# Opening by feature blocks, output projection by token halves, one PSUM pool and a paced residual reload in a two-block transformer kernel

## Chip, cores and metric

One core of a Trainium2 chip runs the whole program. The metric is device time in microseconds (us) of that core for one execution.

## What is computed

Two transformer blocks on one sequence of 512 tokens, 1024 features wide, with a context of 256 tokens. Cut to what bears on the change:

```
# first block (norms are RMS norms, shift and scale come from silu(c) @ ada_w)
h  = norm(x) * (1 + scale1) + shift1          # hc the same from the context
q, k, v, gu, gv, ga, gb = split(h @ w_in)
k_c, v_c = hc @ w_in's columns of k and v
y_a = neighborhood_attention(q, k, v, k_c, v_c)  # 8 heads of 64
y_b = gelu(gu) * (ws @ layernorm(gelu(gv)) + bs) # spatial gating
m  = sigmoid(ga) * (y_a @ w_pa) + sigmoid(gb) * (y_b @ w_pb)
x  = x + g1 * (m @ w_out)
h2 = norm(x) * (1 + scale2) + shift2
# PEER: product keys pick 16 of 16384 experts per head and token
x  = norm(x + g2 * sum_e g_e * gelu(u_e . h2) * v_e)
# second block
x  = x + g * merge(sliding_window_attention(h), retention(h))
x  = x + swiglu(norm(x));  out = norm(x)
```

## The kernel before

Activations lie feature-major: a feature block is 128 features on the partitions by 512 tokens, and there are eight of them. Every float32 product is made of three products of reduced-width parts: `mm3` (L859) multiplies the high part by the high part, the high by the low and the low by the high. `weight` (L850) loads one 512 KB weight from a queue that SyncE (SP) issues in order (L852), splits off its high part on ScalarE (L854) and its low part on VectorE (L856) or, where `pool` is set, on GpSimd. Four raw buffers and three of each part let a weight be issued about six ahead of its use. `split` (L917) does the same for activations. `proj` makes one 512-wide output block from one weight: 8 feature blocks by 3 products, 24 matmuls. A scheduler of the language orders each engine's instructions by priority and readiness; each engine and each DMA queue then runs its list in that order.

**Opening** (`body`, L968 to L1055). The transposed input xT is loaded, `stats` squares it and `rfactor` (L883) makes the norm's factor R1 (Ln, Exp, Square on ScalarE, two VectorE operations nt and nR). The modulation weights adaA come in eight loads of 1 MB, one for each block of *input* features (L969 on), each split in two pieces (ah on ScalarE, al on VectorE). So the sums of all shifts and scales end together, with the last load:

```python
for k in range(KB):
    nc.sync.dma_start(ar, I["adaA"][k])
    ...
        nc.tensor.matmul(a_[:4, :], scp[:, k, :], ah[:, d], start=k == 0, stop=False)
        nc.tensor.matmul(a_[:2, :], scp[:, k, 0:2], al[:, d], start=False, stop=k == KB - 1)
```

Four copies to asb, sixteen transposes, m1 (L989, L990) and s1 (L998) follow, then `modulated` (L940): per feature block md on VectorE (L943), hh on ScalarE (L944), hl on VectorE (L945). The same is done for the context (cT, hc). Only then come the four projections of gv (a gelu on each, L1047, gv transposed at L1057 for the layernorm), then the four of gu.

**Attention** (L1188 to L1227). Four head pairs b, four query blocks each: scores S (L1194, L1195) into two banks, bias and maximum on VectorE, pr = exp on ScalarE (L1200), transposes T (L1203), output O (L1211). A list `beside[b]` names projections that fill TensorE's gaps between these: for b < 3 the next pair's queries, keys and values, and for every b two of the eight `gate` projections (L1071).

**Output projection** (L1246 to L1257). For each of eight output blocks: 24 matmuls, the residual block xr loaded through the ScalarE queue, x1 = acc * g1 + xr (L1255), `squares` (L902), whose sum over features is made by two matmuls with ones (L915). Then `rfactor`, and in `peer` md, hh, hl of h2 (L249 to L251) and the first three query projections together (`proj_many`, L254). x1 is kept in device memory as xs (L256).

**PEER** (`peer`, L137). After the retrieval, for each of 128 groups of experts, 24 hidden-layer matmuls; for the early groups the result `act` is written to device memory (`spilled`, L382) and read back by SP (`fetch`, L448) when its turn to be multiplied by the expert outputs comes (`output`, L427, which splits it as wh and wl and runs 18 matmuls into six banks o_ps). The gate tables (ring), expert weights (raw from in_uT, in_uv) and gathered rows (GpSimd queue) stream beside. `paced` (L159) makes an instruction wait for the output multiplication that was written last. At the end xr, all of xs, is reloaded for the residual (L475), ysb takes the six banks (L480, L482), and `block` (L485) transposes and adds, from about 1771 us on.

**PSUM.** Five pools one after another, each with its own tags and numbers of banks; a pool's banks become free for the next pool when the pool closes.

## Time and profile before

| | |
|---|---|
| median of 3 runs | 2605.16 us (2601.26 to 2610.33) |
| profiled execution's own time | 2605.44 us |
| its span in the trace | 2603.7 us |
| mean granted clock of TensorE | 0.982 |
| TensorE (PE) busy | 2494.0 us, 96% |
| VectorE (DVE) busy | 1793.4 us, 69% |
| ScalarE (ACT) busy | 1057.7 us, 41% |
| GpSimd (POOL) busy | 310.7 us, 12% |

The time of an execution holds 1.7 us around the span. PEld is TensorE's weight loading, which runs beside its matmuls. A row of the time order gives start, duration, engine, line, output and inputs, and in brackets how long the engine had been idle and the instruction that ended it. A window row gives busy times and, behind them, the granted clock of TensorE as a share of 2.4 GHz. All stretches are in us from the start of the span.

### The profile page before, as it was taken

What the parts mean: (1) busy time and instruction counts of PE and PEld (TensorE: products, weight loads), DVE (VectorE), ACT (ScalarE), POOL (GpSimd) and SP (SyncE); (2) the same over time, 40 slices, a digit from 0 to 9 for tenths busy, and PEclk for the clock granted to TensorE, in tenths of its full rate; (3) what the DMA queues carried; (4) which work ended last, traced back from release to release, by engine and by line L of the source; (5) the groups of instructions that cost most, each with busy time, mean ns of one, the idle gap of its engine ahead of it and who ended that gap; (6) DMA issues with size and microseconds to landing.
All of it is one profiled execution on the core that took longest, in us unless ns stands there. A gap on an engine that the chain in (4) does not pass through costs nothing.

```text
span 2603.7 us, 34186 instructions
## 1 busy us (share of the span) xinstructions
PE 2494.0 (96%) x12941; PEld 2128.5 (82%) x12941; DVE 1793.4 (69%) x2999; ACT 1057.7 (41%) x1820; POOL 310.7 (12%) x199
## 2 busy tenths in 40 slices
PE   5899999899899999999989999998999999999998
PEld 2688888689889999999968888886788888888887
DVE  6555655799998888868868888876765334533345
ACT  6424553333335444444433334434533323422343
POOL 1000110002531111122212222210000000000000
PEclk9899999999999999999989999999999999999999
DMA  6353433224677888899998899973112232222254
GB/s 251 109 170 121 146 105 119 85 90 145 214 247 280 300 294 292 293 334 345 332 323 309 312 359 351 362 267 105 57 42 76 94 97 98 96 96 96 95 181 164
DMA packets 145764, 511.24 MB, mean 196 GB/s; under 512 B 13632, under 2 KB 39360, under 8 KB 125888
## 3 DMA queue, kind: packets, MB, share of 16 engines
q1 hardware_dynamic: 114352, 330.14, 37.3%
q0 software_dynamic: 18432, 134.23, 14.2%
q10 hardware_dynamic: 12816, 44.70, 4.6%
q8 instruction: 101, 1.65, 0.3%
q14 instruction: 63, 0.52, 0.1%
HBM read 465.50 MB, written 43.52 MB: 195 GB/s over the span
## 4 chain that ended last, share of the span: by engine, by line
PE 84%; DVE 9%; ACT 2%; issue 1%; DMA 1%; POOL 0%; DVEq 0%; SPq 0%; ACTq 0%; POOLq 0%
PE ps_mm L860 13%; PE ps_mm L861 13%; PE ps_mm L862 13%; PE o_ps L862 6%; PE o_ps L861 6%; PE o_ps L860 6%; PE ps_S L861 3%; PE ps_S L860 3%; PE ps_S L862 3%; PE g_ps L196 3%; DVE lo L856 2%; PE acc L861 2%; PE acc L862 2%; PE acc L860 2%; PE ps_O L1211 1%
## 5 line engine op out<-in xcount | busy, mean ns | idle before, releaser
L856 DVE TENSOR_TENSOR lo<-raw,hi 128x1024 fp32r<-128x1024 f32 x474 | 592.3, 1250 | 388.7 <-ACT hi L854 375.7
L854 ACT ACTIVATE hi<-raw 128x1024 fp32r<-128x1024 f32 x478 | 504.1, 1056 | 775.7 <-PE ps_mm L861 455.9
L860 PE MATMUL ps_mm<-hh,hi 128*128 128x512 f32 (+1 forms) x1776 | 663.4, 375 | 26.7 <-ACT gv L1047 11.9
L862 PE MATMUL ps_mm<-hh,lo 128*128 128x512 f32 (+1 forms) x1776 | 658.7, 371 | 24.2 <-DVE lo L856 24.2
L861 PE MATMUL ps_mm<-hl,hi 128*128 128x512 f32 (+1 forms) x1776 | 660.2, 372 | 2.3 <-DVE hl L919 2.2
L860 PEld LDWEIGHTS ps_mm<-hh,hi 128*128 128x128 f32 x1776 | 337.8, 190 | 66.1 <-ACT gv L1047 12.3
L862 PEld LDWEIGHTS ps_mm<-hh,lo 128*128 128x128 f32 x1776 | 338.5, 191 | 63.9 <-DVE lo L856 27.8
L861 PEld LDWEIGHTS ps_mm<-hl,hi 128*128 128x128 f32 x1776 | 338.2, 190 | 41.3 <-DVE hl L919 3.3
L860 PE MATMUL o_ps<-hi,wh 128*128 128x512 f32 x768 | 300.1, 391 | 12.1 <-ACT wh L918 12.1
L177 POOL DMA_INDIRECT rows<-in_uv,dix x128 | 214.3, 1674 | 763.2 <-DVE act L434 190.0
L862 PE MATMUL o_ps<-hi,wl 128*128 128x512 f32 x768 | 300.4, 391 | 0.4 <-DVE wl L919 0.4
L861 PE MATMUL o_ps<-lo,wh 128*128 128x512 f32 x768 | 300.1, 391 | 0.0
L860 PEld LDWEIGHTS o_ps<-hi,wh 128*128 128x128 f32 x768 | 144.8, 189 | 42.1 <-ACT wh L918 12.5
L862 PEld LDWEIGHTS o_ps<-hi,wl 128*128 128x128 f32 x768 | 144.7, 188 | 32.1 <-DVE wl L919 2.0
L168 DVE SCALAR_TENSOR_TENSOR accn<-rows,wgt,accn 128x1024 f32<-128x1024 f32 x128 | 167.2, 1306 | 5.0 <-ACT wgt L174 3.5
L861 PEld LDWEIGHTS o_ps<-lo,wh 128*128 128x128 f32 x768 | 144.8, 189 | 29.6
L171 DVE SCALAR_TENSOR_TENSOR rows<-rows,hn 128x1024 f32<-128x1024 f32 x128 | 156.5, 1223 | 17.2 <-ACT act L380 8.3
L918 ACT ACTIVATE wh<-act 128x384 fp32r<-128x384 f32 x104 | 54.6, 526 | 256.4 <-PE o_ps L861 239.3
L192 DVE TENSOR_TENSOR gi<-oh,gt 128x1536 bf16<-128x1536 bf16 x96 | 91.3, 954 | 0.9
L190 DVE TENSOR_TENSOR oh<-iob,ji 128x1024 bf16<-128x1024 bf16 x96 | 65.8, 688 | 26.9 <-PE g_ps L196 26.2
L196 PE MATMUL g_ps<-gi,oh 128*128 128x128 bf16 x1152 | 77.5, 219 | 0.0
L196 PEld LDWEIGHTS <-oh 128*128 128x128 bf16 x1152 | 66.1, 97 | 10.4 <-issue 7.7
(400 smaller groups left out, 3530.7 us busy)
## 6 DMA issues: line engine op xcount, KB each, us to landing
raw<-in_uT SPq DMA_DIRECT2D x128, 512.0 KB, 5.0
raw<-in_uv SPq DMA_DIRECT2D x128, 512.0 KB, 6.5
raw<-in_win SPq DMA_DIRECT2D x82, 512.0 KB, 3.4
raw<-in_wd SPq DMA_DIRECT2D x44, 512.0 KB, 3.3
act<-act ACTq DMA_DIRECT2D x52, 384.0 KB, 3.4
act<-act SPq DMA_DIRECT2D x52, 384.0 KB, 7.7
gs<-stage ACTq DMA_DIRECT2D x16, 1152.0 KB, 6.8
ring<-gs SPq DMA_DIRECT2D x12, 1536.0 KB, 13.4
```

What stands on the lines that cost most here:

```text
L168: nc.vector.scalar_tensor_tensor(accn, rows.pop(k - 3)[:, D:], wgt[:, c], accn, op0=ALU.mult, op1=ALU.add)
L171: paced(nc.vector.scalar_tensor_tensor(r[:, :D], r[:, :D], 1.0, hn, op0=ALU.mult, op1=ALU.mult, accum_out=dot[:, c]))
L177: paced(nc.gpsimd.indirect_dma_start(out=r, out_offset=None, in_=I["uv"], in_offset=bass.IndirectOffsetOnAxis(ap=dix[:, k:k + 1], axis=0)))
L190: nc.vector.tensor_tensor(oh, io, each(ji[:, t0 // 4], 2), ALU.is_equal)
L192: nc.vector.tensor_tensor(gi, oh[:, 1].unsqueeze(1).broadcast_to([P, 3, 2, P, 2]), each(gt[:, t0 // 4], 3), ALU.mult)
L196: nc.tensor.matmul(g_ps[:, t, :], oh[:, 0, t // 2, :, t % 2], gi[:, j, t // 2, :, t % 2], start=j == 0, stop=j == 2)
L854: nc.scalar.activation(hi, raw, AF.Copy)
L856: (nc.gpsimd if pool else nc.vector).tensor_sub(lo, raw, hi.bitcast(F32))
L860: nc.tensor.matmul(ps, w[0], x[0], start=first, stop=False)
L861: nc.tensor.matmul(ps, w[0], x[1], start=False, stop=False)
L862: nc.tensor.matmul(ps, w[1], x[0], start=False, stop=last)
L918: nc.scalar.activation(hi, src, AF.Copy)
```

## The change

Five parts:

1. **Opening.** adaA is laid out by *output* feature block: load b now holds the shift and scale columns of feature block b for all input features. `vectors(b)` makes m and s of that block (16 matmuls 256 wide, one copy to asb, two transposes, three small VectorE operations) and modulates that block. The four gv weights are loaded at the start, and their products over feature block b run as soon as it is modulated, into four banks. gv's gelus, gu's projections and only then the context's `stats` and `modulated` follow.
2. **Gates.** The eight gate projections go beside the head pairs as 1, 1, 1 and 5, no longer 2 each.
3. **Output projection.** x1 is preloaded with xT by four loads; blocks 0 to 4 are made whole, blocks 5 to 7 for the first 256 tokens and then for the last 256, each half with its own `rfactor`. `peer` modulates and projects the first three queries by the same halves.
4. **PSUM.** One pool of eight banks for the whole program; `banks` gives each stage's names a set of bank numbers to go round.
5. **Residual reload.** xr comes in eight loads of 256 KB, the first released by the output multiplication sixteenth from the end, the last by the ninth.

```diff
@@ opening
-            for k in range(KB):
-                ar = p0.tile([P, 2 * D], F32, name="ar", bufs=4)
-                nc.sync.dma_start(ar, I["adaA"][k])
...
+            def load(b):
+                ar = p0.tile([P, KB, 2 * P], F32, name="ar", bufs=3)
+                nc.sync.dma_start(ar.rearrange("p k c -> p (k c)"), I["adaA"][b])
...
+            def vectors(b, a):
+                acc = bank("O")[:4, :2 * P]
+                for k in range(KB):
+                    nc.tensor.matmul(acc, scp[:, k, :], a[0][:, k, :], start=k == 0, stop=False)
+                    nc.tensor.matmul(acc[:2], scp[:, k, 0:2], a[1][:, k, :], start=False, stop=k == KB - 1)
...
+                modulated(sp, hh, hl, lambda k: xT[:, k, :], S, s1[:, 0, :], R1, m1[:, 0, 0:8], (b,))
...
+            gv_ps = [bank(tag) for tag in ("mm", "mm", "S", "S")]
+            vectors(0, load(0))
+            wv = [early(16, True), early(17, False)]
+            vectors(1, load(1))
+            wv += [early(18, True), early(19, False)]
+            for b in range(KB):
+                if b + 2 < KB:
+                    a = load(b + 2)
+                c = slice(b * P, (b + 1) * P)
+                for acc, w in zip(gv_ps, wv):
+                    mm3(acc, (w[0][:, c], w[1][:, c]), (hh[:, b, :], hl[:, b, :]), b == 0, b == KB - 1)
+                if b + 2 < KB:
+                    vectors(b + 2, a)
@@ attention
-        for b, (i0, i1) in enumerate(((0, 2), (2, 4), (4, 6), (6, 8))):
+        for b, (i0, i1) in enumerate(((0, 1), (1, 2), (2, 3), (3, 8))):
@@ output projection
-                xr = pm.tile([P, S], F32, tag="xr", name="xr", bufs=2)
-                nc.scalar.dma_start(xr, I["xT"][b])
...
+            for b in range(0, KB, 2):
+                nc.scalar.dma_start(x1[:, b:b + 2, :], I["xT"][b:b + 2].rearrange("k p t -> p k t"))
             for b in range(KB):
+                late.append((b, weight(I["wout"][b])))
+                if b < KB - 3:
+                    wout(*late.pop())
+            for half in HALVES:
+                for a in late:
+                    wout(*a, half)
+                rfactor(sr, ms[:, half], S // 2, into=R[:, half], tag="h")
@@ peer, its entry
+                for c in HALVES:
+                    for k in range(KB):
...
+                    proj_many([q[:, c] for q in q3], wq, (hh[:, :, c], hl[:, :, c]))
@@ peer, its end
-        nc.sync.dma_start(xr, xs.rearrange("k p t -> p k t"))
+        for k in range(KB):
+            paced(nc.sync.dma_start(xr[:, k, :], xs[k]), 2 * KB - k)
@@ PSUM
+        def bank(tag, shape=(P, S)):
+            i = sets[tag][turn[tag] % len(sets[tag])]
+            turn[tag] += 1
+            return psum.tile(list(shape), F32, tag="bank%d" % i, name="ps_" + tag)
```

Three places of the engines' lists. TensorE where the modulation ends and the gv projections (hh, hl by hi, lo) begin, before:

```order
L977 MATMUL ps_mm<-al,scp 2x512 x2
L977 MATMUL ps_S<-al,scp 2x512 x2
L986 MATMUL ps_O<-ident,asb 128x4 x16
L860 MATMUL ps_mm<-hh,hi 128x512 x2
L861 MATMUL ps_mm<-hl,hi 128x512
L862 MATMUL ps_mm<-hh,lo 128x512
```

and after, around the third feature block's sums (L980, L981 are now the modulation's products):

```order
L981 MATMUL ps_O<-al,scp 2x256
L860 MATMUL ps_mm<-hh,hi 128x512 x2
L986 MATMUL ps_T<-ident,asb 128x4 x2
L860 MATMUL ps_S<-hh,hi 128x512 x2
L861 MATMUL ps_mm<-hl,hi 128x512
L862 MATMUL ps_mm<-hh,lo 128x512
...
L861 MATMUL ps_S<-hl,hi 128x512
L862 MATMUL ps_S<-hh,lo 128x512
L980 MATMUL ps_O<-ah,scp 4x256
```

The gv products of one feature block now stand between the modulation products of later blocks. TensorE in the last head pair of the attention, where one query block's scores (S, from kk and qs, qx) are followed by its transposes (T, from pr), before:

```order
L1194 MATMUL ps_S<-kk,qs 128x512
L1195 MATMUL ps_S<-kk,qx 128x512
L1194 MATMUL ps_S<-kk,qs 128x512
L1195 MATMUL ps_S<-kk,qx 128x512
L1203 MATMUL ps_T<-ident,pr 128x128 x8
L1211 MATMUL ps_O<-V_2684,pT 128x64 x8
```

and after, nineteen products of gates (hh, hl) between the scores and the transposes, of which the last six stand here:

```order
L861 MATMUL ps_mm<-hl,hi 128x512
L862 MATMUL ps_mm<-hh,lo 128x512
L860 MATMUL ps_mm<-hh,hi 128x512
L861 MATMUL ps_mm<-hl,hi 128x512
L862 MATMUL ps_mm<-hh,lo 128x512
L860 MATMUL ps_mm<-hh,hi 128x512
L1218 MATMUL ps_T<-ident,pr 128x128 x8
```

Transposes that stood right behind their scores have gate products ahead of them. SP's list where the first spilled act tiles are read back, before:

```order
L852 DMA raw<-in_uv 128x1024 x6
L475 DMA xr<-xs 128x8x512
L448 DMA act<-act_3556 128x768
L448 DMA act<-act_3557 128x768
L448 DMA act<-act_3558 128x768
```

and after, the place near the end of PEER where the eight pieces now stand (at the old place the act loads follow the raw ones directly):

```order
L441 DMA act<-act_3778 128x768
L469 DMA xr<-xs 128x512
L852 DMA raw<-in_uv 128x1024
L469 DMA xr<-xs 128x512 x2
L852 DMA raw<-in_uv 128x1024
L469 DMA xr<-xs 128x512
L441 DMA act<-act_3779 128x768
L852 DMA raw<-in_uv 128x1024
```

The one reload that stood ahead of the first act loads is now eight that alternate with the last weight and act loads.

## Rows read from the trace of the kernel before

**Rows 1.** The page: span, and TensorE's busy time.
```profile
span 2603.7 us, 34186 instructions
...
PE 2494.0 (96%) x12941; PEld 2128.5 (82%) x12941; DVE 1793.4 (69%) x2999; ACT 1057.7 (41%) x1820; POOL 310.7 (12%) x199
```

**Rows 2.** TensorE's waits: total us, times, longest us.
```profile
PE ps_mm L862 <- DVE lo L856: 24.2, 9, 5.1
...
PE o_ps L860 <- ACT wh L918: 12.1, 1, 12.1
...
PE ps_mm L860 <- ACT hh L520: 1.2, 1, 1.2
```

**Rows 3.** Windows of the opening: length, busy of PE, PEld, DVE, ACT, POOL, granted clock, DMA share, GB/s.
```profile
14.50:40.00 25.50, 20.17 (x82) 5.71 (x80) 19.80 (x21) 21.84 (x24) 2.90 (x2) 1.00 0.79 309
40.00:45.80 5.80, 0.00 (x0) 0.00 (x0) 5.73 (x7) 1.18 (x3) 4.46 (x2) 0.60 0.84 263
45.80:61.00 15.20, 13.96 (x48) 10.54 (x48) 12.95 (x23) 9.29 (x17) 0.00 (x0) 0.81 0.20 74
61.00:74.10 13.10, 1.13 (x4) 0.68 (x4) 8.52 (x20) 9.29 (x16) 0.00 (x0) 0.66 0.35 107
74.10:87.30 13.20, 13.17 (x48) 10.64 (x49) 1.23 (x1) 2.03 (x4) 0.00 (x0) 0.82 0.20 72
```

**Rows 4.** VectorE by line and shape, 0 to 75 us: busy us, mean ns, idle before.
```profile
L919 DVE TENSOR_TENSOR al<-ar,ah 128x1024 fp32r<-128x1024 f32 x16 | 18.6, 1221 | 6.2 <-ACT ah L918 6.2
L943 DVE SCALAR_TENSOR_TENSOR md<-xT,s,nR 128x512 f32<-128x512 f32 x8 | 7.6, 997 | 0.0
L945 DVE SCALAR_TENSOR_TENSOR hl<-md,m,hh 128x512 fp32r<-128x512 f32 x8 | 5.5, 743 | 0.0
...
L989 DVE TENSOR_TENSOR m<-ps_O,vec 128x32 f32<-128x32 f32 x1 | 0.2, 193 | 1.2 <-PE ps_O L986 1.2
```

**Rows 5.** ScalarE by line, same stretch.
```profile
L1047 ACT ACT_TABLE_LOAD x1 | 1.3, 1283 | 0.0
```

**Rows 6.** TensorE in order of time: attention of the last head pair.
```profile
386.41 1.97 PE L1203 MATMUL ps_T<-ident,pr 128*128 128x128 f32 x8 [4.05 <-ACT pr L1200]
...
395.86 1.12 PE L1203 MATMUL ps_T<-ident,pr 128*128 128x128 f32 x4 [2.06 <-ACT pr L1200]
```

**Rows 7.** Windows behind the three later stalls.
```profile
388.00:392.00 4.00, 4.00 (x19) 3.69 (x18) 0.26 (x1) 0.60 (x1) 0.00 (x0) 0.50 0.00 0
396.00:400.00 4.00, 4.00 (x20) 3.72 (x20) 0.80 (x2) 1.07 (x3) 0.00 (x0) 0.55 0.02 4
476.00:480.00 4.00, 3.39 (x8) 2.60 (x9) 4.00 (x7) 2.07 (x4) 0.00 (x0) 0.50 0.00 0
1344.00:1348.00 4.00, 4.00 (x10) 3.10 (x10) 2.55 (x4) 0.50 (x2) 0.00 (x1) 0.50 0.84 284
```

**Rows 8.** TensorE in order of time: output projection's end to PEER's first query.
```profile
467.06 0.39 PE L862 MATMUL ps_mm<-mh,lo 128*128 128x512 f32 x1
469.02 1.12 PE L915 MATMUL ps_T<-sq,ones 128*128 128x512 f32 x2 [1.56 <-ACT sq L906]
476.61 1.65 PE L860 MATMUL ps_mm<-hh,hi 128*128 128x512 f32 x3 [6.47 <-ACT hh L250]
```

**Rows 9.** TensorE in order of time: a run of 256-wide products.
```profile
203.16 0.28 PE L860 MATMUL ps_mm<-hc,hi 128*128 128x256 f32 x1
...
205.92 0.28 PE L862 MATMUL ps_mm<-hc,lo 128*128 128x256 f32 x1
```

**Rows 10.** DMA issued 1322 to 1332 us: KB, median us to landing.
```profile
xr<-xs SPq DMA_DIRECT2D x1, 2048.0 KB, 18.2
...
act<-act SPq DMA_DIRECT2D x3, 384.0 KB, 18.5
```

**Rows 11.** The same, issued 1350 to 1740 us.
```profile
act<-act SPq DMA_DIRECT2D x48, 384.0 KB, 7.3
```

**Rows 12.** Window where the last outputs' products run.
```profile
1700.00:1710.00 10.00, 10.00 (x45) 8.28 (x45) 8.41 (x11) 4.59 (x8) 1.80 (x1) 1.00 1.06 390
```

More of the change, by code (lines that the diff above doesn't have):

```diff
@@ L179, in gather, with build @@
                 yield 2.4
-        def build(g0, gs, pool, st):
+        def build(g0, gs, bank, st):
             def each(a, n):
@@ L410, in peer @@
             c6.close()
-            cps.close()
             p2 = c5.enter_context(tc.tile_pool(name="p2", bufs=2, side="right"))
-            cpo = c2.enter_context(ExitStack())
-            po = cpo.enter_context(tc.tile_pool(name="po", bufs=1, space=PSUM))
-            ph = cpo.enter_context(tc.tile_pool(name="ph", bufs=2, space=PSUM))
-            o_ps = [[po.tile([P, S], F32, name="o_ps%d%d" % (n, half)) for half in range(2)] for n in range(DT)]
+            o_ps = [[bank("o") for half in range(2)] for n in range(DT)]
             order = list(range(first, P)) + list(range(first))
@@ L454, in peer @@
                     acts[pos] = tg.tile([P, T], F32, tag="act", name="acf", bufs=AB)
[L455 removed]
+                    hidden(lambda: bank("h"), acts[pos], 0)
                 if pos == P - first - 1:
@@ L491, in peer, with enter_second @@
         return enter(pe, block)
-def enter_second(ctx, tc, I, pool, block, vec, gain, ones, weight, mm3, proj):
+def enter_second(ctx, tc, I, banks, pool, block, vec, gain, ones, weight, mm3, proj):
     nc = tc.nc
@@ L515, in enter_second @@
     w3 = [weight(I["win2"][b]) for b in range(3)]
-    a3, ms = [bank("mm", 3) for _ in range(3)], bank("S", 2)
+    a3, ms = [bank("mm") for _ in range(3)], bank("S")
     for k in range(KB):
-        block(k, X[:, k, :], bank("T", 2))
+        block(k, X[:, k, :], bank("T"))
         g = g12[:, k:k + 1]
@@ L795, in second @@
         for pair in range(2):
-            acc = [[ps.tile([P, S], F32, tag="A", name="acc", bufs=6) for _ in range(2)] for _ in range(2)]
+            acc = [[bank("A") for _ in range(2)] for _ in range(2)]
             def add(i, half, w, b):
@@ L910, in squares @@
         elif k < KB - 1:
-            nc.vector.tensor_add(held["sum"], held["sum"], sq)
+            nc.vector.tensor_add(held["sum"][:, c], held["sum"][:, c], sq)
             if k == KB - 2:
-                nc.tensor.matmul(acc, ones, held["sum"], start=True, stop=False)
+                nc.tensor.matmul(acc, ones, held["sum"][:, c], start=True, stop=False)
         else:
@@ L921, in enter @@
     def enter(pool, block):
-        return enter_second(ctx, tc, I, pool, block, vec, gain, ones, weight, mm3, proj)
+        return enter_second(ctx, tc, I, banks, pool, block, vec, gain, ones, weight, mm3, proj)
     mod = cp.tile([P, 48], F32, name="mod")
@@ L1004, in body @@
-        h = (hh, hl)
-        c1t.close()
+            def load(b):
+                ar = p0.tile([P, KB, 2 * P], F32, name="ar", bufs=3)
+                nc.sync.dma_start(ar.rearrange("p k c -> p (k c)"), I["adaA"][b])
+                ah = p0.tile([P, KB, 2 * P], F32R, name="ah", bufs=2)
+                al = p0.tile([P, KB, 2 * P], F32R, name="al", bufs=2)
+                for q in range(2):
+                    k = slice(q * 4, q * 4 + 4)
+                    split(ah[:, k], al[:, k], ar[:, k])
+                return ah, al
@@ L1032, in body @@
         later = modvecs()
-        sga = pz.tile([P, KB, S], F32, name="sga")
+        cT = pz.tile([P, 2, KB, CTX], F32, tag="sga", name="cT")[:, 0]
+        for k in range(0, KB, 4):
+            nc.sync.dma_start(cT[:, k:k + 4, :], I["cT"][k:k + 4].rearrange("k p t -> p k t"))
         gbm = pz.tile([P, KB, S], F32, name="gbm")
@@ L1040, in body @@
         ybh = pg.tile([P, 2, 4, S], F32R, name="yb")
-        pad(pg, 160)
+        pad(pg, 224)
         gv = pg.tile([P, 4, S], F32, tag="gv", name="gv")
         for b in range(4):
-            w = weight(I["win"][16 + b], pool=b < 3)
-            acc = bank("mm", 2)
+            nc.scalar.activation(gv[:, b, :], gv_ps[b], AF.Gelu_apprx_tanh)
+        sc_ = c1g.enter_context(tc.tile_pool(name="sc", bufs=1, side="right"))
+        gu = pg.tile([P, 4, S], F32, name="gu")
+        for b in range(4):
+            w = weight(I["win"][12 + b])
+            acc = bank("mm")
             proj(acc, w, h)
-            nc.scalar.activation(gv[:, b, :], acc, AF.Gelu_apprx_tanh)
+            nc.scalar.activation(gu[:, b, :], acc, AF.Gelu_apprx_tanh)
         wsT = pg.tile([P, 8, P], F32, name="wsT")
@@ L1061, in body @@
             nc.scalar.activation(gvn[:, n, :], tp, AF.Copy)
-        gu = pg.tile([P, 4, S], F32, tag="gv", name="gu")
-        for b in range(4):
-            w = weight(I["win"][12 + b])
-            acc = bank("mm", 2)
-            proj(acc, w, h)
-            nc.scalar.activation(gu[:, b, :], acc, AF.Gelu_apprx_tanh)
+        Rc = stats(sc_, lambda k: cT[:, k, :], CTX)
+        hch, hcl = hc[:, 0], hc[:, 1]
+        modulated(sc_, hch, hcl, lambda k: cT[:, k, :], CTX, s1[:, 1, :], Rc, m1[:, 1, 0:8])
         Rv = rsqrt(sg, mv[:, :, 1], [P, NT], "rv")
```

259 lines of the change are left out of this document (119 added, 140 removed).

## The prediction

> **What bounds the kernel now.** I read the page's totals first: TensorE is busy 2494.0 of 2603.7 us [rows 1]. A change that takes away no matmul can give back only the 109.7 us in which TensorE stands still, and what its lower clock costs just after. The view of TensorE's waits says where these are [rows 2]: 24.2 us are waits for weights' low parts on VectorE, nearly all in PEER's retrieval, which the change leaves as it is. The other large waits come once each. So I took those stretches one by one, by windows and in order of time, and looked at two things in each: which engine worked while TensorE waited, and the granted clock after the wait.
>
> **Opening [rows 3].** From 40.0 to 87.3 us, 47.3 us, TensorE runs 96 gv products (48 and 48) and little else, though the second 48 took only 13.2 us at a clock of 0.82. It stands for 5.8 us while VectorE makes the first md and for 11.9 of the 13.1 us from 61.0 to 74.1, where the row shows VectorE at 8.5 us and ScalarE at 9.3: the context's modulation and the gelu that frees a bank. Before 40.0 the stretch from 14.5 shows 20.2 us of TensorE in 25.5, VectorE 19.8, ScalarE 21.8: the splitting of adaA sets that pace.
>
> **Attention [rows 6].** In the last head pair the transposes wait 4.05 and 2.06 us for ScalarE's exp; the clock is then 0.50, its lower level of 1.2 GHz, and 0.55 with TensorE full [rows 7].
>
> **Output projection [rows 8].** The last of its products starts at 467.06 (0.39 long); PEER's first query starts at 476.61. Between them stand only two matmuls with ones; ScalarE's squares and the chain norm factor, md, hh make the rest. Then again a clock of 0.50 [rows 7].
>
> **Reload [rows 10].** SP's list puts the 2 MB reload ahead of the first three act loads. It takes 18.2 us to land, and the act loads 18.5, against 7.3 for the 48 act loads after it [rows 11]. The 12.1 us wait for wh [rows 2] is the split of such an act; from 1344 to 1348 the clock is 0.50 [rows 7].
>
> **The change, part by part** (all against the profiled execution's 2605.4 us, which lies 0.3 above the median).
>
> *Opening: -21.* The modulation of a block no longer waits for all eight loads, so the gv products fill TensorE while VectorE splits the next block. VectorE then has, one after another: 16 al, 18.6; md, 8 by 0.743 (I take hl's row; md's own mean of 0.997 holds pieces beside GpSimd's splits); hl, 5.5; three low parts of weights as long as an al, 3.7; 24 small operations by some 0.22 (0.193 in the row, and the step to the next), 5.3; R1's two, 1.5. Together 40.5 us [rows 4]. They start near 13.5 us, since the first al opens the stretch at 14.5 or just ahead of it. With the 6.2 us that the al already wait for ScalarE [rows 4] the last hl ends near 60. Then come 8 more products (1.8), and gu can start when gelu, with its table load of 1.28 [rows 5], has freed a bank and ScalarE has made a high part: some 2.8. That is 64.5, against 87.3: -23. The context's norm and modulation move behind gu. Their cover is gu's 96 products, 22 us at full rate; their 16 half-width operations are some 6 us of VectorE. But the layernorm's small chain queues behind them on VectorE and ScalarE: +2. If that cover is gone they cost those 6. TensorE must also keep up: in a block 12 products and 16 half-width ones, by 0.246 us for a full one in 14.5 to 40 (20.17 us by 82), make 4.9 us in about 5.8. Ends: without the 6.2 us, -27. With every block in a chain of its own (two al 2.4, small ones 0.6, md and hl 1.5, 12 products at the 0.274 of 74.1 to 87.3, 3.3: 7.8 by eight) gu starts at 80 and -7 + 2 = -5 is left.
>
> *Gates: -8.* Between the last pair's scores and transposes now stand 19 gate products, 19 by 0.23 or 4.3 us, where TensorE waited 4.05 [rows 6]. Given back are the 6.1 us of waits and half of the 4 us that run at 0.50 and nearly half of those at 0.55 [rows 7], 3.8: 9.9. The gates are the same eight, so the first three pairs lose one each, 24 products or 5.5 us of cover. The projections of the next pair still stand there, so I charge 2. Ends: -9.9 if that costs nothing, -3.7 if each of the three gets a wait like the 2.06.
>
> *Output projection: -6.5.* From the end of the last product (467.45) to the first query is 9.2 us, of which the ones matmuls are work, some 0.9; half of the 3.39 us at half clock is 1.7. So 10.0 are there to be had. By halves, the norm and modulation of the first 256 tokens run beside the last three blocks' second half, 72 products of 256; those of the second half beside the queries' first half, again 72. Such a product steps by 0.12 us (203.16 to 205.92 holds 23 steps) [rows 9], so either cover is 8.6 us, and the half's chain is at most the 9.2 of the whole and probably two thirds. The price: 144 pairs of half products at 0.24 where one of 512 took 0.227 (the step from 1700 to 1710, 10 us by 45, is 0.222 with its shorter ones), 144 by 0.013 or 1.9. VectorE meets the second half's x1 and nt behind the first half's 16 md and hl, so I leave 1.6 as a wait. The preload of x1 moves eight loads to four earlier ones on ScalarE's queue, which hide under the attention's last products. Ends: -8.1 with no wait left, 0 with the first half waiting as long as the whole does now.
>
> *Reload: -13.* The act loads then land in some 7.3 us after issue, and the 12.1 us wait goes, with half of the 4 us at 0.50, 2.0; I keep 1 us of it as a wait. The eight pieces go to the last sixteen outputs, released by the sixteenth to the ninth from the end. An output's 18 matmuls are 4.0 us (45 in 10 us [rows 12]), so the last piece has 32 us until the sum. There the DMA share is 1.06 at 390 GB/s [rows 12], but TensorE was full in that window. Behind a waiting piece on SP stand weights and acts; they are issued some six outputs, 24 us, ahead of their use, and a landing takes 7.3. Ends: -14, or 0 if the wait is not the reload's doing.
>
> *One PSUM pool: -0.5.* No pool boundary now holds a tile until a whole pool closes. The largest wait at such a place is 1.2 [rows 2]. It has no row of its own before, so I bound it by that: 1.2 either way, for each of the two boundaries behind PEER.
>
> Sum: -21 - 8 - 6.5 - 13 - 0.5 = -49, so 2556.
>
> A rule of the Trainium skill speaks against the pieces. What the rows show: 2 MB in one DMA took 18.2 us in a full stream [rows 10], 384 KB 7.3 in a nearly full one [rows 11], so eight small ones have more landing time between them than one large. "DMA: Bandwidth & Descriptors", section "Bandwidth", says to gather transfers into 1 MiB or more, and its section on the anatomy of one DMA gives each a fixed part of about 2.0 us. By that, as an estimate from this page, eight cost 14 us more than one, and the reload's gain would be gone, which is rival B's first form. No run here shows it; the rows say that nothing needs a piece for 32 us.
>
> **The rivals.**
>
> *A. The opening stays as slow as it is.* In 40.0 to 87.3 the clock was 0.60 to 0.82 [rows 3]. If TensorE, stopped a little in every block, drops to half clock there, a block is 9.8 us of it, and eight from 13.5 end at 92, later than now. More likely it reaches the 80 us of the chain by blocks. With the opening at 0 to -5 the sum is 2577 down to 2572. For it: the order puts gv's products behind the modulation products of later blocks, so one late split holds both. Against it: from 14.5 to 40.0 the clock was 1.00 at much the same share of work.
>
> *B. The reload's gain does not come.* Either the new place has no room, as [rows 12] would let one think (eight pieces in a stream that is full), or the 12.1 us come from the gathers and weights beside it and not from the reload. Then 2605.4 - 36 = 2569. Against it: the act loads took 18.5 us only there [rows 10, 11].
>
> *C. Slower: the pieces hold SP.* SP issues in order. If the weight behind each piece is issued less than one landing before its use, TensorE waits 7.3 us [rows 11] for each of eight: 58 us, more than the 49 gained, so 2614. It decides from a lead of under 7.3 us; by the order and the buffers the lead is about 24.
>
> *D. The change does not do what it says.* The scheduler may leave the new places unused. The rows of the new order show gv's products between the modulation's, gates behind the scores and pieces near the end, so little remains of this; it would give 2600 or more.
>
> **How the numbers follow.** Forecast 0.68, A 0.14, B 0.11, C 0.03, D 0.04. The forecast's own terms spread by their ends over some 2543 to 2570; I take 2541 as the lower end of the range, where the three large terms are all near their best. A alone and B alone lie inside 2585; both together come to it. C and D, and the forecast with several terms at their worst, are the part left out above. A measurement of this kernel can tell about 0.3% from no change, 7.8 us. Faster by more: all but C, D and a little of the others, 0.93; within it 0.04; slower 0.03.
>
> **What the changed profile would show.** Opening: gu's first product near 64 us, gv's gelus just before, no wait of TensorE above 2 us after 20, a clock near 1.00. Attention: no wait above 1.5 us for pr, clock at 1.00 in the last pair. Output projection: the first query within 2 us of the last half product, half products stepping by 0.12. Reload: no 12 us wait for wh; the first act loads land in about 7; the eight pieces land before the last output, and TensorE has no gap there. The prediction is wrong where one of these has a new wait of 5 us or more, above all a wait for weights among the last sixteen outputs, or a clock under 0.9 in the opening.

## The result, and the profile after

The changed kernel takes 2567.37 us (median of 4 runs, 2567.0 to 2568.37), before 2605.43 (4 runs): a ratio of 0.9854, 95% interval 0.9836 to 0.9871. That is 38.1 us faster where 49 were forecast; the time lies inside the range.

The page of the changed kernel (compare [rows 1]): TensorE is busy for as long as before, and its share has grown because the span is shorter.

```profile
span 2565.2 us, 34641 instructions
...
PE 2487.4 (97%) x13153; PEld 2137.1 (83%) x13153; DVE 1795.4 (70%) x3041; ACT 1066.7 (42%) x1844; POOL 307.2 (12%) x198
```

TensorE's largest waits after (total, times, longest), to be set beside [rows 2]. The 12.1 us for wh is gone; the 24.2 us for low parts, nearly all in the retrieval, have become 28.8; the wait for gv has gone from 11.9 to 2.4; those for ah and yb are new at this size.

```profile
PE ps_mm L862 <- DVE lo L856: 28.8, 5, 9.2
...
PE ps_O L980 <- ACT ah L918: 4.0, 1, 4.0
PE ps_S L860 <- ACT yb L918: 4.0, 1, 4.0
...
PE ps_mm L860 <- ACT gv L1058: 2.4, 1, 2.4
...
PE ps_mm L860 <- ACT hh L248: 2.0, 1, 2.0
...
PE ps_T L1218 <- ACT pr L1215: 1.3, 3, 0.7
```

Where the time went, by the start of a matmul that both traces have (us):

| mark | before | after | gained up to here | in this stretch |
|---|---|---|---|---|
| first attention score | 206.39 | 199.07 | 7.3 | 7.3 |
| first output projection product | 422.71 | 403.81 | 18.9 | 11.6 |
| first gate table product (behind the retrieval) | 790.27 | 770.47 | 19.8 | 0.9 |
| first expert output product | 1138.22 | 1117.49 | 20.7 | 0.9 |
| last expert output product | 1769.65 | 1733.62 | 36.0 | 15.3 |
| last matmul | 2594.30 | 2556.07 | 38.2 | 2.2 |

The reload and the gates gave more than forecast; the opening and the halves fell short. Traces of one and the same opening differ by up to 2.7 us at the first of these marks (196.70 to 199.40 in runs below that leave it as it is), so smaller differences of marks say nothing.

**Opening.** Windows of the changed kernel (columns as in [rows 3]):

```profile
13.50:30.00 16.50, 8.75 (x38) 3.96 (x36) 11.44 (x13) 12.08 (x16) 5.03 (x2) 0.68 0.68 267
30.00:48.00 18.00, 17.99 (x103) 12.72 (x103) 15.21 (x27) 11.81 (x16) 0.00 (x0) 0.91 0.81 306
48.00:62.00 14.00, 14.00 (x81) 10.12 (x79) 10.10 (x18) 6.72 (x10) 0.00 (x0) 1.00 0.21 76
62.00:70.00 8.00, 5.56 (x25) 4.02 (x24) 4.36 (x7) 4.70 (x6) 0.00 (x0) 1.00 0.12 23
...
106.00:118.00 12.00, 12.00 (x76) 9.41 (x75) 11.83 (x26) 6.86 (x13) 0.00 (x0) 1.00 0.14 45
118.00:127.00 9.00, 5.15 (x34) 3.67 (x32) 8.22 (x13) 3.38 (x5) 0.00 (x0) 0.91 0.31 101
127.00:140.00 13.00, 12.76 (x45) 9.90 (x46) 6.94 (x8) 1.12 (x2) 0.00 (x0) 0.80 0.39 129
```

From 30 to 62 us TensorE is full: now it is the bound there. In 13.5 to 30 it is busy for 8.75 of 16.5 us, at a granted clock of 0.68. VectorE is held up by it: the first row here (by line, 0 to 70 us) has 7.0 us in which VectorE waits for TensorE's transposes of shifts and scales, the second (in order of time) is the last hl, which ends at 65.2.

```profile
L989 DVE TENSOR_TENSOR m<-ps_T,vec 128x4 f32<-128x4 f32 x8 | 1.3, 164 | 7.0 <-PE ps_T L986 7.0
...
64.47 0.75 DVE L942 SCALAR_TENSOR_TENSOR hl<-md,m,hh 128x512 fp32r<-128x512 f32 x1 [0.79 <-ACT hh L941]
```

Behind gu, from 118 to 127, TensorE stands for nearly 4 us and runs at 0.80 afterwards. These are the waits at gu's first product and at yb's first product, in order of time (TensorE):

```profile
69.96 0.50 PE L860 MATMUL ps_mm<-hh,hi 128*128 128x512 f32 x1 [2.44 <-ACT gv L1058]
...
127.12 1.22 PE L860 MATMUL ps_S<-yb,hi 128*128 128x512 f32 x2 [3.96 <-ACT yb L918]
```

gu's products start at 69.96, which is 17.4 us ahead of 87.3, but at the first attention score 10 of these are gone. VectorE in order of time, in the spatial gating, shows what is late:

```profile
94.08 1.30 DVE L1077 BATCH_NORM_STATS2 st<-ps_T 128x6 f32<-128x512 f32 x2 [2.59 <-PE ps_T L1075]
...
99.22 0.17 DVE L872 TENSOR_SCALAR rs_a<-mv 128x4 f32<-128x4 f32 x1
...
102.61 1.00 DVE L1093 TENSOR_SCALAR vn<-gvn,mv,rs_R 128x512 f32<-128x512 f32 x2
104.95 0.69 DVE L1099 TENSOR_TENSOR ybt<-ps_T,vec 128x512 f32<-128x512 f32 x1 [1.34 <-PE ps_T L1096]
...
113.45 1.27 DVE L942 SCALAR_TENSOR_TENSOR hc<-md,m,hc 128x256 fp32r<-128x256 f32 x3
114.64 0.88 DVE L940 SCALAR_TENSOR_TENSOR md<-cT,s,nR 128x256 f32<-128x256 f32 x2
115.43 0.69 DVE L1099 TENSOR_TENSOR ybt<-ps_T,vec 128x512 f32<-128x512 f32 x1
...
127.72 0.69 DVE L919 TENSOR_TENSOR yb<-ybt,yb 128x512 fp32r<-128x512 f32 x1
```

gv's statistics (L1077) begin at 94, because the change wrote gv's transposes behind gu; before, the first transposes ran at 87.3, at gu's start, and the statistics began at 89.5. So they come 4.5 us later than before, though gu starts 17.4 us earlier. After them come the layernorm's factor (99 to 102.6), vn and ybt, with the context's md and hc (L940, L942) standing between the gating's operations up to 117. The last yb ends past 128.

**Attention.** The windows that answer to [rows 7] and [rows 6]: full, at full clock.

```profile
381.00:390.00 9.00, 9.00 (x43) 7.27 (x42) 5.85 (x8) 3.72 (x5) 0.00 (x0) 1.00 0.65 234
390.00:396.00 6.00, 6.00 (x28) 4.99 (x27) 5.28 (x8) 2.23 (x3) 0.00 (x0) 1.00 0.26 90
```

**Output projection.** TensorE in order of time, which answers to [rows 8]: the first query product starts 1.6 us after the start of the last output product, where it was 9.5 before; a wait of 1.95 for hh comes 5 us later.

```profile
449.52 0.28 PE L862 MATMUL ps_mm<-mh,lo 128*128 128x256 f32 x1
...
451.15 0.47 PE L860 MATMUL ps_mm<-hh,hi 128*128 128x256 f32 x1
...
456.44 0.79 PE L860 MATMUL ps_mm<-hh,hi 128*128 128x256 f32 x2 [1.95 <-ACT hh L248]
```

ScalarE in the same stretch shows why: the norm factor of the second half loads its two tables (L886, L887) ahead of the first half's next hh (L248).

```profile
452.50 1.28 ACT L886 ACT_TABLE_LOAD   x1
...
454.28 1.28 ACT L887 ACT_TABLE_LOAD   x1
...
455.90 0.49 ACT L248 ACTIVATE hh<-md,mod 128x256 fp32r<-128x256 f32 x1
```

The windows show the price of the halves (107 matmuls in 13.5 us, of which nearly all are half products) and that the clock drops once more, to 0.78:

```profile
436.00:449.50 13.50, 13.49 (x107) 13.00 (x106) 5.21 (x11) 7.49 (x12) 0.00 (x0) 1.00 0.16 39
456.50:464.00 7.50, 7.50 (x50) 7.50 (x51) 7.50 (x20) 4.07 (x11) 0.00 (x0) 0.78 0.01 2
```

**Reload.** SyncE's queue in order of time: the pieces go between the last weights, the first of them 65 us ahead of the residual sum at 1735.

```profile
1670.10 0.38 SPq L469 DMA_DIRECT2D xr<-xs  x1
1671.41 0.33 SPq L852 DMA_DIRECT2D raw<-in_uv  x1
1671.79 0.90 SPq L469 DMA_DIRECT2D xr<-xs  x2
```

### The profile page after: what moved, and what is told of

It is laid out like the page before. It is cut to its first block, busy times and chain, and to the rows that moved or that the text cites. A ratio compares the mean times of both kernels' runs of the same rounds, so it can differ in the third digit from the quotient of the medians.

```text
span 2565.2 us, 34641 instructions
## 1 busy us (share of the span) xinstructions
PE 2487.4 (97%) x13153; PEld 2137.1 (83%) x13153; DVE 1795.4 (70%) x3041; ACT 1066.7 (42%) x1844; POOL 307.2 (12%) x198
## 4 chain that ended last, share of the span: by engine, by line
PE 85%; DVE 10%; ACT 2%; issue 1%; DMA 1%; POOL 0%; DVEq 0%; SPq 0%; ACTq 0%; POOLq 0%
PE ps_mm L860 13%; PE ps_mm L862 13%; PE ps_mm L861 12%; PE ps_o L862 7%; PE ps_o L861 7%; PE ps_o L860 7%; PE ps_S L860 3%; PE ps_S L861 3%; PE ps_S L862 3%; PE ps_S L197 3%; DVE lo L856 2%; PE ps_A L861 2%; PE ps_A L862 2%; PE ps_A L860 2%; PE ps_h L862 1%
## 5 line engine op out<-in xcount | busy, mean ns | idle before, releaser
L854 ACT ACTIVATE hi<-raw 128x1024 fp32r<-128x1024 f32 x474 | 500.0, 1056 | 752.3 <-PE ps_mm L861 423.8
L862 PE MATMUL ps_mm<-hh,lo 128*128 128x512 f32 (+2 forms) x1784 | 655.4, 368 | 28.9 <-DVE lo L856 28.8
L860 PE MATMUL ps_mm<-hh,hi 128*128 128x512 f32 (+2 forms) x1784 | 662.0, 372 | 7.6 <-ACT gv L1058 2.4
L861 PE MATMUL ps_mm<-hl,hi 128*128 128x512 f32 (+2 forms) x1784 | 655.5, 368 | 2.5 <-DVE hl L919 2.2
L861 PEld LDWEIGHTS ps_mm<-hl,hi 128*128 128x128 f32 x1784 | 339.6, 190 | 38.2 <-DVE hl L919 3.3
L862 PE MATMUL ps_o<-hi,wl 128*128 128x512 f32 x768 | 299.5, 390 | 0.4 <-DVE wl L919 0.4
L860 PE MATMUL ps_o<-hi,wh 128*128 128x512 f32 x768 | 298.9, 389 | 0.7 <-ACT wh L918 0.7
L861 PE MATMUL ps_o<-lo,wh 128*128 128x512 f32 x768 | 299.2, 390 | 0.0
L862 PEld LDWEIGHTS ps_o<-hi,wl 128*128 128x128 f32 x768 | 144.2, 188 | 31.4 <-DVE wl L919 1.4
L860 PEld LDWEIGHTS ps_o<-hi,wh 128*128 128x128 f32 x768 | 144.2, 188 | 30.4 <-ACT wh L918 1.0
L861 PEld LDWEIGHTS ps_o<-lo,wh 128*128 128x128 f32 x768 | 144.2, 188 | 29.4
L197 PE MATMUL ps_S<-gi,oh 128*128 128x128 bf16 x1152 | 78.1, 219 | 0.0
```

The source lines that it names most:

```text
L197: nc.tensor.matmul(g_ps[:, t, :], oh[:, 0, t // 2, :, t % 2], gi[:, j, t // 2, :, t % 2], start=j == 0, stop=j == 2)
L854: nc.scalar.activation(hi, raw, AF.Copy)
L860: nc.tensor.matmul(ps, w[0], x[0], start=first, stop=False)
L861: nc.tensor.matmul(ps, w[0], x[1], start=False, stop=False)
L862: nc.tensor.matmul(ps, w[1], x[0], start=False, stop=last)
```

## The experiments

Each starts from the changed kernel unless it says otherwise, and is compared with the kernel before on the same chip. The kernel before took 2604.2 to 2606.2 us (medians) beside them, so times are compared directly with 2567.4; differences of 2 us or less are not told apart.

### The opening undone

```diff
-            gv_ps = [bank(tag) for tag in ("mm", "mm", "S", "S")]
-            vectors(0, load(0))
...
+            am = [bank(tag) for tag in ("mm", "mm", "S", "S")]
+            for k in range(KB):
+                ar = p0.tile([P, 2 * D], F32, name="ar", bufs=4)
...
```

> The changed kernel with the opening of before (modulation weights by input blocks, gv after all modulation, context's norm ahead of gv) and its other four parts kept. My forecast's term for the opening was 21 us: then this run takes 2567.4 + 21 = 2588. The two traces at hand give less: gu starts 17.4 us earlier in the changed kernel (69.96 for 87.32), but the first attention score only 7.3 us earlier (199.07 for 206.39). By that theory (most of the gain is given back in the spatial gating) this run takes 2574 to 2576, with gu's first product near 87 and the first attention score near 206.

Measured: 2577.09 us, ratio to before 0.9883 (0.9863 to 0.9903). The opening is worth 9.7 us, not 21. The first attention score stands at 206.57, as before the change.

### The context's modulation behind the gating

```diff
-        Rc = stats(sc_, lambda k: cT[:, k, :], CTX)
-        hch, hcl = hc[:, 0], hc[:, 1]
-        modulated(sc_, hch, hcl, lambda k: cT[:, k, :], CTX, s1[:, 1, :], Rc, m1[:, 1, 0:8])
         Rv = rsqrt(sg, mv[:, :, 1], [P, NT], "rv")
...
             gate(gbm[:, n, :], 28 + n)
             next(later, None)
+        Rc = stats(sc_, lambda k: cT[:, k, :], CTX)
+        hch, hcl = hc[:, 0], hc[:, 1]
+        modulated(sc_, hch, hcl, lambda k: cT[:, k, :], CTX, s1[:, 1, :], Rc, m1[:, 1, 0:8])
```

> The changed kernel with the context's norm and modulation written behind the spatial gating's four token tiles instead of ahead of the layernorm's factor. Theory 1 (the context's 16 VectorE operations and its ScalarE table loads stand in the queues ahead of the gating's own, so yb is late): the 3.96 us wait for yb at 127.1 goes, the clock of 0.80 behind it (13 us, 2.6 us lost) too, and the time falls by 5 to 7 us to about 2561. Theory 2 (yb is late because gv's transposes and statistics now stand behind gu): the wait stays at 3 us or more and the time is within 1.5 us of 2567.4.

Measured: 2571.91 us, ratio 0.9863 (0.9843 to 0.9883): 4.5 us slower than the changed kernel. Neither theory said this. The wait for yb did go (its first product starts at 122.31, not 127.12), but two others came. TensorE in order of time:

```profile
134.10 0.50 PE L860 MATMUL ps_mm<-hh,hi 128*128 128x512 f32 x1 [3.22 <-ACT hi L854]
...
141.76 1.55 PE L1038 MATMUL ps_O<-one,modacc 128*128 128x2 f32 x8 [1.98 <-DVE modacc L1032]
```

and ScalarE, which splits a weight (hi, L854) only after the context's hc, for which it waits on VectorE's md:

```profile
131.79 1.31 ACT L941 ACTIVATE hc<-md,m 128x256 fp32r<-128x256 f32 x3 [1.07 <-DVE md L940]
133.00 1.04 ACT L854 ACTIVATE hi<-raw 128x1024 fp32r<-128x1024 f32 x1
```

So the context can't be put just anywhere: at a place where weights are split one by one it holds the next one up.

### The layernorm ahead of gu

```diff
+        for n in range(NT):
+            tp = bank("T")
...
+            nc.scalar.activation(gvn[:, n, :], tp, AF.Copy)
         gu = pg.tile([P, 4, S], F32, name="gu")
         for b in range(4):
...
             nc.scalar.activation(gu[:, b, :], acc, AF.Gelu_apprx_tanh)
-        for n in range(NT):
-            tp = bank("T")
...
```

> The changed kernel with gv's transposes and the layernorm's statistics written ahead of gu's projections, as before the change, and the context's norm and modulation left where the change put them. Theory 2 (late layernorm): the wait for yb goes and the time falls by 5 to 7 us to about 2561. Theory 1 (context in the queues): the context still stands between the gating's operations, the wait stays at 2 us or more and the time is 2565 to 2568.

Measured: 2561.90 us, ratio 0.9828 (0.9809 to 0.9848): 5.5 us faster than the changed kernel, as theory 2 said. The context stays where the change put it, and still the wait for yb is gone; the windows that had a wait and a clock of 0.80 are full at 1.00:

```profile
118.00:127.00 9.00, 9.00 (x41) 7.45 (x40) 5.16 (x7) 2.29 (x3) 0.00 (x0) 1.00 0.38 117
127.00:140.00 13.00, 13.00 (x66) 10.74 (x65) 8.59 (x11) 3.18 (x3) 0.00 (x0) 1.00 0.71 225
```

The first attention score is at 191.60, 14.8 us ahead of before.

### The projection whole

```diff
-            for half in HALVES:
-                for a in late:
-                    wout(*a, half)
-                rfactor(sr, ms[:, half], S // 2, into=R[:, half], tag="h")
+            R = rfactor(sr, ms, S, keep=mid)
...
-                for c in HALVES:
+                for c in (slice(0, S),):
```

> The changed kernel with the output projection, its norm, PEER's modulation and first queries over all 512 tokens at once again (the preload of x1 kept). My forecast's term was 6.5 us: 2574. By the marks of the two traces the halves gave 2.6 us up to the first retrieval stall (95.36 us for 92.81 us from the first output product on) and 0.9 up to the first gate table product behind the retrieval: then 2568 to 2570, with a wait of about 6 us before PEER's first query back in the trace. If the halves cost as much as they give, 2566 to 2567.

Measured: 2571.64 us, ratio 0.9866 (0.9847 to 0.9885): the halves are worth 4.3 us. TensorE's waits in this run:

```profile
PE ps_mm L862 <- DVE lo L856: 25.6, 11, 5.1
...
PE ps_mm L860 <- ACT hh L248: 6.5, 1, 6.5
```

The 6.5 us before the first query are back, but the waits for low parts of weights, nearly all in the retrieval, are 25.6 where the changed kernel has 28.8. From the first output product to the first gate table product the run takes 366.8 us (401.46 to 768.26) and the changed kernel 366.7. So what the halves give before the retrieval, the retrieval takes back. In the trace the loss shows up later: 2.0 up to the first expert output (a wait for wh of 2.76 there, in the changed kernel 0.71) and 2.4 up to the last (618.6 for 616.1). But the runs below and above that keep the halves and the paced pieces take 616.1 to 618.3 for this last stretch, so the 2.4 can't be put down to the halves. Why the wait for wh differs was not tested: how the halves gain 4.3 us is not shown.

### Two gates beside each head pair

```diff
-        for b, (i0, i1) in enumerate(((0, 1), (1, 2), (2, 3), (3, 8))):
+        for b, (i0, i1) in enumerate(((0, 2), (2, 4), (4, 6), (6, 8))):
```

> The changed kernel with two gate projections beside each head pair again. My forecast's term was 8 us: 2575. By the marks of the two traces (first attention score to first output product, 216.3 us before and 204.7 after) it is 11.6: 2579, with waits for pr of 4 and 2 us and a clock of 0.50 back in the last pair. If the move only shifts waits between pairs: within 2 us of 2567.

Measured: 2581.41 us, ratio 0.9903 (0.988 to 0.9927): the gates are worth 14.0 us, not 8. Its four runs spread from 2576.5 to 2584.2, so this is 9 to 17. Both waits are back,

```profile
380.67 1.79 PE L1218 MATMUL ps_T<-ident,pr 128*128 128x128 f32 x8 [4.41 <-ACT pr L1215]
...
389.85 1.11 PE L1218 MATMUL ps_T<-ident,pr 128*128 128x128 f32 x4 [2.05 <-ACT pr L1215]
```

and the clock is 0.50 for 16 us, from 382 to 398 (the first and the last of these windows):

```profile
382.00:386.00 4.00, 4.00 (x20) 3.74 (x19) 0.26 (x1) 0.60 (x1) 0.00 (x0) 0.50 0.00 0
394.00:398.00 4.00, 4.00 (x16) 3.51 (x16) 0.69 (x1) 0.00 (x0) 0.00 (x0) 0.50 0.20 38
```

The 14 us that TensorE works in these 16 cost 7; I had allowed 3.8. With the two waits, 6.5, that is 13.5. The trace is of the slowest of the four runs, so this is an upper reading; before and after the change, the stretch from the first attention score to the first output product differs by 11.6.

### The reload as before

```diff
-        for k in range(KB):
-            paced(nc.sync.dma_start(xr[:, k, :], xs[k]), 2 * KB - k)
+        nc.sync.dma_start(xr, xs.rearrange("k p t -> p k t"))
```

> The changed kernel with the residual reloaded by one 2 MB transfer that nothing paces, as before. My forecast's term was 13 us: 2580. By the marks (first output product to the last: 631.4 us before, 616.1 after) it is 15.3: 2582 to 2583, with a wait for wh of about 12 us back. Rival B (the wait is due to gathers and weights, not to the reload): 2567 to 2569.

Measured: 2581.17 us, ratio 0.9908 (0.9887 to 0.9929): the reload is worth 13.8 us. The wait is back:

```profile
1321.35 0.79 PE L859 MATMUL ps_o<-hi,wh 128*128 128x512 f32 x1 [10.37 <-ACT wh L917]
```

### One paced transfer, and pieces without the pace

```diff
-            paced(nc.sync.dma_start(xr[:, k, :], xs[k]), 2 * KB - k)
+        paced(nc.sync.dma_start(xr, xs.rearrange("k p t -> p k t")), 2 * KB)
```

> The changed kernel with the residual reloaded by one 2 MB transfer, released by the output multiplication sixteenth from the end: the new place without the pieces. If the place does it: 2567 within 2 us, either way, and no wait of TensorE above 1 us in the last sixteen outputs. If the pieces matter (one large transfer holds the weights and acts behind it, as it did at the old place): a wait of several us among the last outputs and 2572 to 2580.

Measured: 2570.62 us, ratio 0.9867 (0.9847 to 0.9888). That is 3.2 us slower than the changed kernel, where the expectation for the new place allowed 2; behind the transfer TensorE waits twice for wl, 1.3 us in all.

```diff
-            paced(nc.sync.dma_start(xr[:, k, :], xs[k]), 2 * KB - k)
+            nc.sync.dma_start(xr[:, k, :], xs[k])
```

> The changed kernel with the eight pieces of the reload, unpaced, which stand at the old place among the first act loads: the pieces without the new place. If the place does it: a wait for wh of 8 us or more back in the trace and 2576 to 2583. If cutting it up is enough, since the act loads no longer stand behind 2 MB: 2567 to 2570.

Measured: 2569.69 us, ratio 0.9865 (0.9845 to 0.9886). Either half of part 5 gives 11 us or so of the 13.8, and no wait of TensorE above 1 us is left between the first and the last expert output in either. In the second run the scheduler itself put the pieces between later weights and acts, over 34 us, so no load stands behind 2 MB. In the first a weight is issued 1.3 us behind the 2 MB and an act 7.7 us behind; at the old place three acts followed within 5 us. What makes the new place harmless to one large transfer (the gap to the next act, or how early that act is issued) was not told apart.

### The second adaA block ahead of the gv weights

From the run with the layernorm first:

```diff
             vectors(0, load(0))
-            wv = [early(16, True), early(17, False)]
             vectors(1, load(1))
-            wv += [early(18, True), early(19, False)]
+            wv = [early(16, True), early(17, False), early(18, True), early(19, False)]
```

> The run with the layernorm first (2561.9 us), and in it the second block of adaA loaded and split ahead of the four gv weights instead of between them. In the changed kernel TensorE waits 4.01 us for ah at 22.2 and 1.15 and 2.04 us for al up to 27.7, while ScalarE splits gv weights and VectorE stands idle for 6.7 us between 11.3 and 20.7. If the order of these early splits is what starts gu 5.5 us later than I forecast (69.96 for 64.5), gu starts 3 to 5 us earlier and the time is 2557 to 2559. If VectorE's sum of work sets it anyway, or the gv weights are then late instead: within 1.5 us of 2561.9.

Measured: 2562.80 us, ratio 0.9841 (0.9823 to 0.9858): no gain. TensorE's wait for ah fell from 4.01 to 2.54 us, and the first gv product now waits longer, at the end of the row:

```profile
31.50 1.22 PE L860 MATMUL ps_mm<-hh,hi 128*128 128x512 f32 x2 [4.99 <-ACT hh L941]
```

because two operations on VectorE ahead of the first md, made beside the two low parts on GpSimd, are stretched: the norm factor's nR, 0.68 us in the changed kernel, and one low part, 1.22 us alone (VectorE in order of time):

```profile
23.88 2.87 DVE L892 SCALAR_TENSOR_TENSOR nR<-nt,nr 128x512 f32<-128x512 f32 x1
26.67 3.36 DVE L1002 TENSOR_TENSOR lo<-raw,hi 128x1024 fp32r<-128x1024 f32 x1
```

### The same, with nothing on GpSimd

```diff
-            wv = [early(16, True), early(17, False), early(18, True), early(19, False)]
+            wv = [early(16, False), early(17, False), early(18, False), early(19, False)]
```

> The same with the two low parts that GpSimd makes put on VectorE. In the changed kernel one al beside GpSimd's lo took 3.39 us for 1.22. If GpSimd holds VectorE up by about as much as it takes over (2.2 us more on one al, 1.2 us of work taken over for each of two), this run is equal to the one with the order alone within 1.5 us; if the hold is the larger, 2 us faster and no al over 1.3 us; if the work taken over is the larger, 2 us slower.

Measured: 2560.47 us, ratio 0.9834 (0.9817 to 0.9852), 2.3 us faster than the run before it, by the medians; the two sets of four runs overlap (2559.2 to 2563.3 and 2561.2 to 2563.8), so the gain is not shown by the times. The traces point the same way: the last hl of the opening ends at 63.4 for 68.3. All four low parts are on VectorE now, at 1.22 us each:

```profile
L1002 DVE TENSOR_TENSOR lo<-raw,hi 128x1024 fp32r<-128x1024 f32 x4 | 4.9, 1220 | 0.0
```

It has the lowest median of this study, 6.9 us below the changed kernel; against the layernorm alone (2561.9) the difference can't be told apart.

### The context between the statistics and gu

From the run with the layernorm first, the two statements for Rc and the context's `modulated` stand ahead of gu:

```diff
+        Rc = stats(sc_, lambda k: cT[:, k, :], CTX)
+        hch, hcl = hc[:, 0], hc[:, 1]
+        modulated(sc_, hch, hcl, lambda k: cT[:, k, :], CTX, s1[:, 1, :], Rc, m1[:, 1, 0:8])
         gu = pg.tile([P, 4, S], F32, name="gu")
...
-        Rc = stats(sc_, lambda k: cT[:, k, :], CTX)
-        hch, hcl = hc[:, 0], hc[:, 1]
-        modulated(sc_, hch, hcl, lambda k: cT[:, k, :], CTX, s1[:, 1, :], Rc, m1[:, 1, 0:8])
         Rv = rsqrt(sg, mv[:, :, 1], [P, NT], "rv")
```

> The run with the layernorm first (2561.9 us), and the context's norm and modulation written between the statistics and gu, so that its VectorE work lies beside gu's 22 us. If the context still costs something where it stands (between the gating's operations), 2 to 3 us faster: 2559 to 2560. If the layernorm's place was all of it: 2561 to 2563. If its five table loads and its 7 us of VectorE now hold up gu's weights: 2565 or more.

Measured: 2561.20 us, ratio 0.9833 (0.9815 to 0.985): the same as without it. With the layernorm ahead of gu, the context costs nothing that can be told where the change put it.

### The pool alone

The opening, gates, halves and reload undone as in the runs above, all four together; of the halves and the reload:

```diff
-                rfactor(sr, ms[:, half], S // 2, into=R[:, half], tag="h")
+            R = rfactor(sr, ms, S, keep=mid)
...
-            paced(nc.sync.dma_start(xr[:, k, :], xs[k]), 2 * KB - k)
+        nc.sync.dma_start(xr, xs.rearrange("k p t -> p k t"))
```

> The changed kernel with the opening, the gates, the projection by halves and the paced reload all undone: what is left of the change is the one PSUM pool, and the preload of x1. My forecast's term was 0.5 us faster than before, with 3 either way at most. Undone one by one, the four parts cost 9.7, 14.0, 4.3 and 13.8 us, 41.8 together, more than the 38 us that the change gave. If their gains simply add, the pool alone is 3.8 us slower than before, 2609. If the pool saves the 1.4 us that the marks show from the first ysb transpose to the end, and the single losses overlap, 2603 to 2604, faster than before by 1 to 2 us.

Measured: 2605.49 us, ratio 1.0000 (0.9991 to 1.0009): the pool and the preload together give nothing, within 2.3 us. The single losses, 41.8 together, are 3.7 more than the whole gain of 38.1. They may overlap; with a spread of 8 us in the gates' run alone, that is not shown.

## Why the prediction came out as it did

| part | forecast | shown by undoing it |
|---|---|---|
| opening | 21 | 9.7 |
| gates | 8 | 14.0 |
| output projection by halves | 6.5 | 4.3 |
| reload | 13 | 13.8 |
| pool | 0.5 | 0.0 (alone, with the preload of x1) |
| sum | 49 | 38.1 measured for all |

**Reload: right**, in mechanism and size. Rival B is ruled out in both forms: the reload at its old place brings the wait back, and the new place has room. The Trainium skill's rule that I weighed ("DMA: Bandwidth & Descriptors", section "Bandwidth", larger transfers are the cheaper ones) would have made the pieces the worse choice. The Trainium skill gives the figures that I took from that page, the fixed part of 2.0 us among them, for transfers that GpSimd issues; SyncE issues these. The measurement decides: at the paced place the eight pieces are 3.2 us faster than one transfer (2567.4 for 2570.6), not 14 slower, and unpaced they take 2569.7. TensorE does not wait for them. Rival C is ruled out too: between the first and the last expert output TensorE waits 0.4 us once, at the start.

**Gates: right mechanism, too small.** The 14.0 lie outside the ends that I gave (3.7 to 9.9), and so do the 11.6 by the marks. The term that was mis-sized is the clock: I gave back 3.8 us for the two windows I quoted and left out what lies between and ahead of them. The kernel before shows it:

```profile
386.40:402.00 15.60, 13.53 (x61) 11.69 (x62) 4.24 (x8) 3.27 (x8) 0.00 (x0) 0.58 0.01 3
```

TensorE works 13.53 us there at 0.58, which costs some 5.7; with the 6.1 of waits that is 11.8. The run with the gates undone has 16 us at 0.50. The charge of 2 us for cover lost in the first three pairs was not needed: the changed kernel's waits for pr are 1.3 us in the whole attention.

**Opening: two steps failed.** The first is "VectorE then has, one after another ... the last hl ends near 60". The work is as I summed it: VectorE is busy for 39.4 us from its first al to the last hl, for 40.5. But it stands for some 13 us in between, where I allowed 6.2, and 7.0 of these are waits for TensorE; the last hl ends at 65.2. TensorE is the bound: it is full from 30 to 62 us because it had stood for half of 13.5 to 30 and then started at a reduced clock. At 30 it had made the sums of two of the eight blocks and begun gv's products at 29.1. My check that TensorE keeps up (4.9 us of work in 5.8 per block) took a full clock and no arrears. gu started at 69.96 for 64.5: 5.5 us. The prediction named a clock under 0.9 in the opening as a sign that it is wrong, and 0.68 up to 30 us is that sign. All this is read from the trace and not tested: reordering the early splits moved the waits and gave nothing, and with GpSimd's share on VectorE as well, 1.4 us, which can't be told from nothing. Rival A (TensorE stopped a little in every block, at half clock) did not come: the stops lie ahead of 30 us, and from there on the clock is 0.91 and 1.00.

The second is the "+2" for what moved behind gu. I named the context. But the change moved gv's transposes and statistics behind gu as well, which I did not cost, and the runs tell the two apart: the layernorm put back gave 5.5 us with the context left in place, while the context moved away cost 4.5. Either move takes away the wait for yb; only the layernorm's brings no new one. Between gu's start and the first attention score the changed kernel lost 10 us of its lead, where 2 were forecast; the layernorm's place is 7.5 of these by the marks (191.60 for 199.07) and 5.5 by the time. With it the opening would be worth 15.2 of the 21, and the 5.8 that are left are about the 5.5 by which gu starts late.

**Halves: the price was mis-sized and the gain taken back.** From the first output product to the wait behind the queries (518.07 before, 496.62 after) the halves gave 2.6 us. Waits fell by 5.1 us (8.0 to 3.0), but the same products took 2.5 us longer, where I had charged 1.9 and counted 1.7 of clock as given back; the clock still falls, to 0.78. After that the retrieval, where VectorE is busy for 253 of the 270 us from 500 to 770, takes back what TensorE brings to it. I had read from [rows 2] that the change leaves those waits as they are; they rose by 4.6 us. The 4.3 us by the times lie near the forecast, but no run shows that they come by the mechanism that I gave.

**Pool: nothing**, inside the bounds given. The run holds the preload of x1 too, so neither shows a gain.

The sign and the range held; the time came out 11 us above the forecast because the largest term was half as large as its sum of VectorE work made it. It came no further off because of luck: the opening and the halves fell 13.5 us short, and the gates, outside their own bounds, and the reload gave 6.8 more.

## What to carry to other kernels

When work is overlapped, redo the bound for every engine over the whole stretch, the one that was waiting included: it starts late, at a lower clock, and may be the next bound. List everything that changes sides of a stage, not just what the change speaks of: here gv's transposes and statistics decided more than the sixteen operations that I had watched. And a gain ahead of a stretch that another engine paces should be counted only as far as that stretch. For a low clock, take the whole stretch that shows it and not sample windows.

## What the runs showed of the hardware

VectorE's 128x1024 subtraction takes 1.22 us alone. With a subtraction on GpSimd beside it, it took 3.36 us in the run with the second adaA block ahead and 3.39 in the changed kernel:

```profile
24.22 3.39 DVE L919 TENSOR_TENSOR al<-ar,ah 128x1024 fp32r<-128x1024 f32 x1
```

Handing GpSimd two of the four splits brought nothing: the median is 2.3 us higher than with all on VectorE (2562.80 for 2560.47), with runs that overlap. The Trainium skill says why one of them stands still: by "SBUF — State Buffer", section "Who interferes with whom", VectorE and GpSimd share a pair of ports under an exclusive lock, and a VectorE instruction with two inputs in SBUF contends with a GpSimd instruction that reads SBUF. The trace agrees: the 3.39 us begin 0.07 us behind the start of GpSimd's 2.37 us, and end 1.1 us behind its end.

After a stop of 4.41 us in the attention (the run with two gates beside each pair) TensorE ran at 0.50 for 16 us, a second stop of 2.05 us among them, so 6.5 us of stops cost some 13.5. After waits of 1.00 and 1.95 us around the first queries it was 0.78 over the next 7.5 us. A stop is priced with what comes behind it.
